# Rotating 96 images by 180 degrees: from three equal groups of images to five unlike ones

## The chip, the cores and the metric

The kernel runs on one core of one Trainium2 chip. The metric is the device time of one execution in microseconds (us); the median of several runs is given. A profile is one further execution, taken by the hardware profiler, with a time of its own.

## The reference

The input is 32 x 3 images of 256 x 256 float32 values, 25.17 MB. The output is each image turned by 180 degrees, so nothing is calculated: every byte is moved once.

```python
batch, c, h, w = 32, 3, 256, 256

def reference(x: np.ndarray) -> np.ndarray:
    return np.rot90(x, k=2, axes=(-2, -1)).astype(np.float32)
```

If an image is seen as one list of 65,536 values, turning it by 180 degrees is reversing that list.

## The kernel before

The 96 images are taken as three groups of 32. A group is a tile of 128 rows (the partitions of SBUF) by 16,384 columns: each image is cut into four segments of 16,384 values, and each segment is one row of 64 KB. The three tiles are called `A`, `Bt` and `Ct`; together they hold the whole input in SBUF, so every byte is loaded once, turned in place and stored once.

Reversing an image has two parts. The values within each row are reversed by VectorE. The four rows of an image change places (row 0 with row 3, row 1 with row 2); that is done by the store, which writes the segments of each image to DRAM in backward order (`[:, ::-1, lo:hi]`, line 58).

VectorE reverses a row by swapping columns from both ends (`swap`, lines 61 to 65): up to `J` = 2,048 columns from the right end are copied backward into the scratch tile `T`, the matching columns from the left are copied backward into the right end, and `T` is copied to the left end. So each swap is three copies, all recorded at line 52 (`copy`), and in the profile they show as `T<-A`, `A<-A` and `A<-T`. `turn(t, lo, hi)` repeats this for a range of columns of the left half. The copies keep the order in which they are written.

DMAs are issued from two queues: SP's (`nc.sync`), which carries nearly everything, and ACT's (`nc.scalar`), which loads `Bt` only. Loads are all recorded at line 55 and stores at line 58. The order is written out by hand at the end of the function:

- lines 69 to 71: `A` and `Ct` are loaded by SP, `Bt` by ACT, each as a whole;
- lines 80 and 81: `A` is turned but for its last 2,048 columns of the half; then a small store of `A` is issued, 256 columns (`LEAD`) of each row, 128 KB in all;
- lines 82 to 84: the first 1,008 columns (`MID`) of `Bt` are turned, then the rest of `A`, and the rest of `A` is stored;
- lines 85 to 88: the rest of `Bt` is turned and stored, then `Ct` is turned and stored.

All stores are issued by SP, in this order, each after VectorE has finished the columns it reads. A store has two sides. The side in SBUF is 128 rows. The side in DRAM is a list of three levels: images, segments of an image in backward order, and columns. In the built program it has the form 32x4x256 for the small store, 32x4x16128 for the rest of `A`, and 32x4x16384 for `Bt` and `Ct`. The side in DRAM of a load is 128 rows in order.

Of the kernel before, what the change touches and what calls it, by code (L numbers as in the profile page):

```python
# [2 lines left out]

os.environ.setdefault("NEURON_RT_ULTRASERVER_MODE", "4")

# [4 lines left out]


@with_exitstack
def kernel(
    ctx: ExitStack,
    tc: tile.TileContext,
    x: bass.AP,
    out: bass.AP,
):

    nc = tc.nc
    P = 128

    B, C, H, W = x.shape
    L = H * W
    G = 32
    E = L // 4
    J = E // 8

    x4 = x.rearrange("b c h w -> (b c) (h w)").rearrange(
        "(g n) (s e) -> g (n s) e", n=G, s=4)
    o4 = out.rearrange("b c h w -> (b c) (h w)").rearrange(
        "(g n) (s e) -> g n s e", n=G, s=4)  # L40

    pool = ctx.enter_context(tc.tile_pool(name="slots", bufs=1))
    A = pool.tile([P, E], x.dtype, tag="A")
    Bt = pool.tile([P, E], x.dtype, tag="B")
    Ct = pool.tile([P, E], x.dtype, tag="C")
    T = pool.tile([P, J], x.dtype, tag="T")

    def back(t, lo, hi):
        return t[:, hi - 1:(lo - 1 if lo else None):-1]

    def copy(dst, src):
        tc.keep_in_program_order(nc.vector.tensor_copy(out=dst, in_=src))  # L52

    def load(t, g, lo, hi, queue=nc.sync):
        return queue.dma_start(out=t[:, lo:hi], in_=x4[g][:, lo:hi])

    def store(t, g, lo, hi):
        return nc.sync.dma_start(
            out=o4[g][:, ::-1, lo:hi], in_=t[:, lo:hi])

    def swap(t, lo, w):
        hi = E - lo - w
        copy(T[:, 0:w], back(t, hi, hi + w))
        copy(t[:, hi:hi + w], back(t, lo, lo + w))
        copy(t[:, lo:lo + w], T[:, 0:w])

    MID = 1008
    LEAD = 256
    load(A, 0, 0, E)
    load(Bt, 1, 0, E, nc.scalar)  # L70
    load(Ct, 2, 0, E)

    def turn(t, lo, hi):
        while lo < hi:
            w = min(J, hi - lo)
            swap(t, lo, w)
            lo += w

    half = E // 2
    turn(A, 0, half - J)  # L80
    store(A, 0, 0, LEAD)
    turn(Bt, 0, MID)
    turn(A, half - J, half)
    store(A, 0, LEAD, E)
    turn(Bt, MID, half)
    store(Bt, 1, 0, E)
    turn(Ct, 0, half)
    store(Ct, 2, 0, E)


# [1 line left out]
_INS = ['x']  # L92
_OUTS = [((32, 3, 256, 256), 'float32')]


# [23 lines left out]
```

## Time and profile before

| | |
|---|---|
| median of 3 runs | 121.99 us (121.83 to 122.44) |
| the profiled execution, its own time | 122.31 us |
| its span, first to last instruction | 120.5 us |
| VectorE busy | 44.7 us (37%), 39 copies |
| moved by DMA | 50.33 MB in 1,008 packets, mean 418 GB/s |
| small store of `A`: issued, landed after | 45.77 us, 16.3 us |
| rest of `A`: issued | 59.28 us |

How to read it: times are counted from the start of the span. The page cuts the span into 40 equal slices of 3 us and prints one digit for each: the share of the slice, in tenths, in which an engine was busy; for DMA it is the mean of the core's 16 DMA engines. The rows of the DMA queues (`q1` is SP's, `q10` is ACT's) say how many packets and bytes each carried, and how much of 16 engines' time over the span they took. The rows of the issues say for each transfer which tile it writes from which (`out_dram<-A` is a store of `A`), its size where the page has it, and the time from issue to landing. An issue to landing contains all the time that the transfer waits in the queue behind earlier ones. A row of 64 KB makes one packet, and the 112 packets under 512 B carry no data of the images but close the transfers.

### The profile page before, as it was taken

The page shows a single profiled execution, that of the slowest core. Times are in us where ns is not written, and L with a number is a line of the kernel's source. Part 1 is how long each engine was busy: PE and PEld are TensorE (multiplying, and loading weights), DVE is VectorE, ACT ScalarE, POOL GpSimd, SP SyncE. Part 2 cuts the span into 40 slices and gives each one's busy share as a digit, 9 for nine tenths or more (in the row PEclk, how much of TensorE's full clock was granted, in tenths as well). Part 3 has the DMA queues.
Part 4 walks back from the last instruction along what each step waited for, and adds up shares of the span by engine and source line. Part 5 has one row for each costly group of instructions (what it writes and reads, how often), then busy time and mean ns, then how long its engine had stood idle before and what let it go on. Part 6 is the DMA issues. An engine that isn't in the chain of part 4 may idle for free.

```text
span 120.5 us, 96 instructions
## 1 busy us (share of the span) xinstructions
DVE 44.7 (37%) x39; POOL 0.2 (0%) x4
## 2 busy tenths in 40 slices
DVE  0000000000000099999999999999910000000000
POOL 0000000000000000000000000000000000000000
DMA  9888988898889888988999977988898889888980
GB/s 348 348 348 370 674 348 348 370 652 370 348 370 652 370 348 348 674 370 348 348 386 599 428 343 343 664 369 348 348 674 370 348 348 674 370 348 348 674 370 0
DMA packets 1008, 50.33 MB, mean 418 GB/s; under 512 B 112, under 2 KB 240, under 8 KB 240
## 3 DMA queue, kind: packets, MB, share of 16 engines
q1 hardware_dynamic: 864, 41.94, 81.3%
q10 hardware_dynamic: 144, 8.39, 16.1%
HBM read 25.17 MB, written 25.17 MB: 418 GB/s over the span
## 4 chain that ended last, share of the span: by engine, by line
DVE 37%; DMA 34%; issue 1%
DMA A<-in_x_dram 34%; DVE T L52 12%; DVE Bt L52 9%; DVE A L52 8%; DVE Ct L52 8%
## 5 line engine op out<-in xcount | busy, mean ns | idle before, releaser
L52 DVE COPY T<-A 128x2048 f32<-128x2048 f32 x4 | 4.9, 1227 | 42.1 <-DMA A<-in_x_dram 42.0
L52 DVE COPY Bt<-T 128x2048 f32<-128x2048 f32 (+2 forms) x5 | 5.1, 1014 | 0.2
L52 DVE COPY T<-Bt 128x2048 f32<-128x2048 f32 (+2 forms) x5 | 5.1, 1014 | 0.2
L52 DVE COPY Bt<-Bt 128x2048 f32<-128x2048 f32 (+2 forms) x5 | 5.1, 1013 | 0.2
L52 DVE COPY T<-Ct 128x2048 f32<-128x2048 f32 x4 | 4.9, 1228 | 0.1
L52 DVE COPY A<-T 128x2048 f32<-128x2048 f32 x4 | 4.9, 1227 | 0.1
L52 DVE COPY Ct<-T 128x2048 f32<-128x2048 f32 x4 | 4.9, 1227 | 0.1
L52 DVE COPY Ct<-Ct 128x2048 f32<-128x2048 f32 x4 | 4.9, 1227 | 0.1
L52 DVE COPY A<-A 128x2048 f32<-128x2048 f32 x4 | 4.9, 1226 | 0.1
L103 POOL MEMSET const-bfloat16-1.0<- 128x1 bf16 x1 | 0.1, 101 | 0.0
L103 POOL MEMSET const-uint8-127<- 128x1 uint8 x1 | 0.1, 101 | 0.0
L103 POOL MEMSET const-float32-0.0<- 128x1 f32 x1 | 0.1, 98 | 0.2 <-issue 0.2
L103 POOL MEMSET const-float32-1.0<- 128x1 f32 x1 | 0.1, 98 | 0.0
## 6 DMA issues: line engine op xcount, KB each, us to landing
out_dram<-A SPq DMA_DIRECT2D x1, 8064.0 KB, 21.9
out_dram<-A SPq DMA_DIRECT2D x1, 128.0 KB, 16.3
Bt<-in_x_dram ACTq DMA_DIRECT2D x1, 41.4
A<-in_x_dram SPq DMA_DIRECT2D x1, 41.2
Ct<-in_x_dram SPq DMA_DIRECT2D x1, 60.5
out_dram<-Bt SPq DMA_DIRECT2D x1, 27.6
out_dram<-Ct SPq DMA_DIRECT2D x1, 31.8
```

The costliest lines, as they stand in the source:

```text
L52: tc.keep_in_program_order(nc.vector.tensor_copy(out=dst, in_=src))
L103: nc = _bacc.Bacc("TRN2", target_bir_lowering=False, num_devices=1)
```

## The change

The three equal groups become five unlike ones, of 8, 32, 32, 16 and 8 images, called `a` to `e`. Each group is again a tile of 128 rows, so an image of `a` and `e` is cut into 16 rows of 4,096 values (16 KB), one of `b` and `c` into 4 rows of 16,384 (64 KB), and one of `d` into 8 rows of 8,192 (32 KB). In the profile all five tiles are called `tile`.

The loads are issued in the order `a` (SP), `e` (ACT), `b`, `c`, `d` (SP). VectorE turns `a`, `e`, most of `b` (all but the last 1,152 columns of its half), the first 2,912 columns of `c`, the end of `b`, the rest of `c`, and `d`. The stores are issued in the order `b`, `c`, `d`, `a`, `e`, all by SP and each as a whole; there is no small store ahead of them. In the built program the DRAM sides of the stores have the forms 32x4x16384 (`b`, `c`), 16x8x8192 (`d`) and 8x16x4096 (`a`, `e`); the SBUF sides are 128 rows. VectorE has 42 copies instead of 39. `J` is 2,048 as before.

```diff
-    MID = 1008
-    LEAD = 256
-    load(A, 0, 0, E)
-    load(Bt, 1, 0, E, nc.scalar)
-    load(Ct, 2, 0, E)
+    class Group:
+        def __init__(self, name, first, count):
+            rows = P // count
+            self.width = L // rows
+            self.tile = pool.tile([P, self.width], x.dtype, tag=name)
+            self.source = images[first:first + count].rearrange(
+                "n (s e) -> (n s) e", s=rows)
+            self.target = turned[first:first + count].rearrange(
+                "n (s e) -> n s e", s=rows)
+
+        def load(self, queue):
+            queue.dma_start(out=self.tile[:, :], in_=self.source)
+
+        def store(self):
+            nc.sync.dma_start(out=self.target[:, ::-1, :], in_=self.tile[:, :])
...
-    half = E // 2
-    turn(A, 0, half - J)
-    store(A, 0, 0, LEAD)
-    turn(Bt, 0, MID)
-    turn(A, half - J, half)
-    store(A, 0, LEAD, E)
-    turn(Bt, MID, half)
-    store(Bt, 1, 0, E)
-    turn(Ct, 0, half)
-    store(Ct, 2, 0, E)
+    counts = (("a", 8), ("b", 32), ("c", 32), ("d", 16), ("e", 8))
...
+    a.load(nc.sync)
+    e.load(nc.scalar)
+    b.load(nc.sync)
+    c.load(nc.sync)
+    d.load(nc.sync)
+
+    LAST = 1152
+    MID = J + 864
+    half = b.width // 2
+    a.turn(0, a.width // 2)
+    e.turn(0, e.width // 2)
+    b.turn(0, half - LAST)
+    c.turn(0, MID)
+    b.turn(half - LAST, half)
+    b.store()
+    c.turn(MID, half)
+    c.store()
+    d.turn(0, d.width // 2)
+    d.store()
+    a.store()
+    e.store()
```

More of the change, by code (lines that the diff above doesn't have):

```diff
@@ L32, with turn @@
     L = H * W
[L33 to L40, printed above, removed]
+    J = L // 32
+    images = x.rearrange("b c h w -> (b c) (h w)")
+    turned = out.rearrange("b c h w -> (b c) (h w)")
     pool = ctx.enter_context(tc.tile_pool(name="slots", bufs=1))
-    A = pool.tile([P, E], x.dtype, tag="A")
-    Bt = pool.tile([P, E], x.dtype, tag="B")
-    Ct = pool.tile([P, E], x.dtype, tag="C")
     T = pool.tile([P, J], x.dtype, tag="T")
+    class Group:
[11 more added lines that the diff above has]
+            nc.sync.dma_start(out=self.target[:, ::-1, :], in_=self.tile[:, :])
+        def turn(self, lo, hi):
+            while lo < hi:
+                w = min(J, hi - lo)
+                swap(self.tile, self.width, lo, w)
+                lo += w
     def back(t, lo, hi):
@@ L52, in copy, with swap @@
         tc.keep_in_program_order(nc.vector.tensor_copy(out=dst, in_=src))
[L54 to L62, printed above, removed]
+    def swap(t, width, lo, w):
+        hi = width - lo - w
         copy(T[:, 0:w], back(t, hi, hi + w))
@@ L65, in swap @@
         copy(t[:, lo:lo + w], T[:, 0:w])
-    MID = 1008
-    LEAD = 256
-    load(A, 0, 0, E)
-    load(Bt, 1, 0, E, nc.scalar)
-    load(Ct, 2, 0, E)
[L73 to L77, printed above, removed]
-    half = E // 2
-    turn(A, 0, half - J)
-    store(A, 0, 0, LEAD)
-    turn(Bt, 0, MID)
-    turn(A, half - J, half)
-    store(A, 0, LEAD, E)
-    turn(Bt, MID, half)
-    store(Bt, 1, 0, E)
-    turn(Ct, 0, half)
-    store(Ct, 2, 0, E)
+    counts = (("a", 8), ("b", 32), ("c", 32), ("d", 16), ("e", 8))
+    groups, first = [], 0
+    for name, count in counts:
+        groups.append(Group(name, first, count))
+        first += count
+    a, b, c, d, e = groups
+    a.load(nc.sync)
[18 more added lines that the diff above has]
+    e.store()
 _INS = ['x']
```

## The prediction

> **What bounds the kernel now.** I read the page from its second part down: how busy each engine and the DMA are over time, then what the DMA queues carried, then when each DMA was issued and when it landed, and last the trace's busy time by stage. The page first: the DMA row and the packet totals, the two queues, and the issues.
>
> ```profile
> DVE  0000000000000099999999999999910000000000
> ...
> DMA  9888988898889888988999977988898889888980
> ...
> DMA packets 1008, 50.33 MB, mean 418 GB/s; under 512 B 112, under 2 KB 240, under 8 KB 240
> ...
> q1 hardware_dynamic: 864, 41.94, 81.3%
> q10 hardware_dynamic: 144, 8.39, 16.1%
> ...
> out_dram<-A SPq DMA_DIRECT2D x1, 8064.0 KB, 21.9
> ...
> Bt<-in_x_dram ACTq DMA_DIRECT2D x1, 41.4
> A<-in_x_dram SPq DMA_DIRECT2D x1, 41.2
> Ct<-in_x_dram SPq DMA_DIRECT2D x1, 60.5
> out_dram<-Bt SPq DMA_DIRECT2D x1, 27.6
> out_dram<-Ct SPq DMA_DIRECT2D x1, 31.8
> ```
>
> VectorE works in the middle third only (44.7 us of 120.5). The DMA digits are 8 or 9 almost from edge to edge, and the queue shares add up to 81.3 + 16.1 = 97.4% of sixteen engines' time. So the kernel is bound by bytes over sixteen DMA engines, and only 3 us of the span are not their work. The next view is busy time by stretches (columns: stretch, length, VectorE, GpSimd, clock, DMA share, GB/s). A share above 1 in a short stretch comes from whole packets counted where they start.
>
> ```profile
> 0.00:1.70 1.70, 0.00 (x0) 0.20 (x4) 1.00 0.00 0
> ...
> 80.30:99.60 19.30, 7.44 (x7) 0.00 (x0) 1.00 0.99 428
> 99.60:118.90 19.30, 0.00 (x0) 0.00 (x0) 1.00 0.99 431
> 118.90:120.50 1.60, 0.00 (x0) 0.00 (x0) 1.00 0.01 0
> ```
>
> The store stages stand at 0.99; what is idle is 1.7 us at the start and 1.6 at the end. The third view is the timeline, which has the issue times (start, length, instruction):
>
> ```profile
> 41.99 1.23 DVE L52 COPY T<-A 128x2048 f32<-128x2048 f32 x1 [41.99 <-DMA A<-in_x_dram]
> 43.25 1.23 DVE L52 COPY A<-A 128x2048 f32<-128x2048 f32 x1
> ...
> 72.84 0.54 SPq L58 DMA_DIRECT2D out_dram<-Bt  x1
> ...
> 87.98 0.54 SPq L58 DMA_DIRECT2D out_dram<-Ct  x1
> ```
>
> Issue plus time to landing gives the stages. Ct's load, issued at 1.18, lands at 61.7: that is the whole of the reading, 25.17 MB. A's large store, issued at 59.28, lands at 81.2; Bt's at 72.84 + 27.6 = 100.4; Ct's at 87.98 + 31.8 = 119.8. So 8.39 MB of stores take 19.3 us on sixteen engines, 2.3 us per MB. From the last landing to the profiled execution's 122.31 us are 2.5 us. The chain of waits names A's load and then VectorE, but that is the chain by releasers; the DMA never runs dry behind it.
>
> **Loads, part by part.** The bytes are the same: 8 + 32 + 32 + 16 + 8 images make 25.17 MB in and out. Loads go out in the order a (SP) beside e (ACT), then b, c, d. Before, 16.78 MB in two queues had landed at 42.0, from a first movement at 1.7: 2.4 us per MB. So a and e, 4.19 MB, land at about 12, b at 31, c at 51, d at 61 to 62. Nothing of this moves the end of reading: 61.7 stays. One more issue ahead of b on SP (0.4 us each) happens while a moves.
>
> **VectorE.** It has 42 copies instead of 39, over the same number of elements. A 128x2048 copy repeats every 1.26 us (43.25 - 41.99). The turns: a 3.8 and e 3.8 us (done by 20); b's first part 9 x 1.26 plus three copies of 896 at about 0.65 (the 1008 ones take 0.69) = 13.3, from 31 to 45; c's first part 3.8 + 1.9 = 5.7, from 51 to 57; b's last 1152 columns 3 x 0.80 = 2.4, to 59 to 60. Then b's store is issued. Its cover is the end of reading: before, SP issued the first load at 0.73 and nothing moved until 1.7, so about 1 us of start makes 60 to 61, against a last landing of 61.7. It just fits; each us that this store came later would be a us at the end. I take 0, with 0 to +0.8. c's turn is done near 69 and needed at 81, d's near 77 and needed at 100; a and e were ready long before. VectorE's earlier start therefore buys nothing: no DMA waits for it.
>
> **The removed lead store.** It is 128 rows of 1 KB. Reading's end to A's landing is 81.2 - 61.7 = 19.5 us, against 19.3 for an unsplit store: the lead costs 0.2 us, and goes.
>
> **Shorter rows.** Loads and stores of a and e are 512 rows of 16 KB where 128 of 64 KB were; those of d 256 of 32 KB where 128 were: 512 rows more. If a row more costs what the lead's did (0.2 us for 128), that is 0.8; if the bytes alone count, 0. Eight KB and more stand nearer to the 64 KB rows than to 1 KB, so I take 0.2. With the lead's 0.2 this cancels.
>
> **The stores of a and e.** All depends on this part. In the built order the last two stores have the form 8x16x4096, d's is 16x8x8192, those of b and c 32x4x16384. Every DMA of before has an outermost count of 32 or 128, and 112 packets under 512 B for seven DMAs is 16 each: one closing packet on each of sixteen engines. So a list with a multiple of 16 at its head is seen to be spread over sixteen. A list that begins with 8 isn't in the trace. Bounds: if the 128 rows are dealt out all the same, a and e take 4.19 / 8.39 x 19.3 = 9.65 us, and the cost is 0. If each outer entry goes to one engine, eight engines carry what sixteen did: 19.3 us, or +9.65. A gain is excluded, since sixteen engines at 0.99 are the most there is. A further end: two streams that share a path take twice as long (A and Bt shared the engines up to 42 and landed together at 42, while 8.39 MB alone take 19.3). Should the eight engines be slowed so as well, it is 38.6 us, or +28.95. Nothing hides any of this: a and e are last, and both would sit on the same eight engines, so engines that ended d's share early find no more work. I take +9.65: all that the trace has is even shares of whole outer entries, eight entries make eight such shares, and 16 KB rows ran nowhere at half speed.
>
> [...]
>
> [...]
>
> **The sum.** Reading ends at 61.7; b 19.3 and c 19.3; d 9.65; that is 110.0. Then a and e 19.3: 129.3. With the 2.5 us of the end, 131.8 for an execution that corresponds to the profiled 122.31. That one is 0.3 above the median of 121.99, so **131.5**.
>
> **Rivals.**
>
> *Sixteen engines after all* (not slower). The rows are dealt out whatever the list looks like. For it: all seven DMAs of before ended on sixteen engines, though their lists differ (32 and 128). Against it: both are multiples of 16. It decides if the two last stores close with 16 small packets each. Then 110.0 + 9.65 + 2.5 - 0.3 = 121.9, with 121.3 to 122.8 by the small terms: the DMA was full before and is full after. Chance 0.13.
>
> *Eight engines, each at half speed.* For it: streams on one path do halve each other, as A and Bt did. Against it: before, all sixteen engines together ran stores at 428 to 431 GB/s without loss, so no shared path below that is seen. 110.0 + 38.6 + 2.5 - 0.3 = 150.8; with a part of the slowing, anything between 132 and 151. Chance 0.23.
>
> *d's store suffers too*, its 16 entries being slowed like the eight: another 9.65, 141 to 160. For it speaks only that 16 is a new count; it is a multiple of 16. Chance 0.05.
>
> **How the numbers follow.** The forecast, eight engines at full speed, has 0.59; its own range is 130.5 to 133 (row and cover terms of -0.4 to +1.4). Range 130 to 152: it holds the forecast, the halving and what lies between; left out are the sixteen engines (0.13) and the worst of d (some 0.04). What a measurement can tell from no change is 0.5%, 0.6 us. Faster by more than that needs the sixteen engines and a row cost of nothing: 0.03. Within it, the rest of that rival: 0.10. Slower: 0.87.
>
> **What would show it.** In the changed kernel's profile: b's store issued at 59 to 60 and landed near 81, c's near 100, d's near 110; first copy near 12; the two last landings about 9.65 us apart, the last near 129; the DMA row at 9 up to about 110 and at 4 to 5 for some 19 us after it. Packets under 512 B: 8 x 16 + 2 x 8 = 144 with eight engines, 160 with sixteen. DMA digits of 2 in the end would mean the halving; a b store that lands well after 81, a lost cover. The prediction is wrong if the last stretch stands at 9, or if the time is lost before a's store begins.

## The result and the profile after

The changed kernel takes 148.76 us (median of 4 runs, 148.70 to 150.18), the kernel before 122.22 us beside it (4 runs, 121.83 to 122.68). The ratio is 1.221, with a 95% interval of 1.216 to 1.226: slower by 26.5 us, where 9.5 were forecast. The profiled execution took 148.77 us, its span is 147.0.

The page of the changed kernel, in the order in which the page of before was read:

```profile
DVE  0004950019994099999990000000000000000000
...
DMA  5999998979696999996969696969699945444530
...
DMA packets 1424, 50.33 MB, mean 342 GB/s; under 512 B 144, under 2 KB 144, under 8 KB 144
...
q1 hardware_dynamic: 1280, 48.24, 84.2%
q10 hardware_dynamic: 144, 2.10, 3.5%
...
out_dram<-tile SPq DMA_DIRECT2D x1, 4096.0 KB, 42.7
out_dram<-tile SPq DMA_DIRECT2D x2, 2048.0 KB
```

A slice is now 3.7 us. VectorE begins at 13 us instead of 42 and is done by 77: its part went as planned. The DMA row stays high up to slice 32, about 118 us, and then falls to 4 and 5: half of the engines are idle. There are 144 small packets for ten transfers, 8 x 16 + 2 x 8: two transfers closed on eight engines. These two print no time to landing on the page, but the completion events in the trace have it: `a` landed at 135.4 us and `e` at 146.1.

The place of the loss is plainer in the stretches (columns: stretch, length, VectorE, GpSimd, clock, DMA share, GB/s):

```profile
80.40:100.00 19.60, 0.00 (x0) 0.00 (x0) 1.00 1.03 435
100.00:110.00 10.00, 0.00 (x0) 0.00 (x0) 1.00 0.94 197
110.00:119.00 9.00, 0.00 (x0) 0.00 (x0) 1.00 1.01 233
119.00:128.00 9.00, 0.00 (x0) 0.00 (x0) 1.00 0.51 149
128.00:137.00 9.00, 0.00 (x0) 0.00 (x0) 1.00 0.49 188
137.00:146.00 9.00, 0.00 (x0) 0.00 (x0) 1.00 0.31 129
```

The first line is the store of `c`: sixteen busy engines, 435 GB/s. The next two are the store of `d`: the share says that all sixteen engines are as busy as before, but they move half as much. That is the reading to take from this page: **share and rate have to be read together**, because an engine counts as busy for the whole of a slow packet. The 32 KB packets of `d` took 2.52 us here (median); in `flat_all`, an experiment below that stores `d` at full rate, they took 1.21. The last three lines are `a` and `e`: half of the engines, and at first less than half of the rate.

Landings say the same. These are the issues of `c` and `d` and the time to landing of `c`; that of `d`, 42.7, is on the page above:

```profile
69.78 0.56 SPq L55 DMA_DIRECT2D out_dram<-tile  x1
out_dram<-tile SPq DMA_DIRECT2D x1, 30.9
77.35 0.57 SPq L55 DMA_DIRECT2D out_dram<-tile  x1
```

The store of `b` is issued at 59.78 and lands 21.3 later, at 81.1; that of `c` lands at 69.78 + 30.9 = 100.7; that of `d`, issued at 77.35, at 120.05. So `d` took 19.4 us, where 4.19 MB of `b` or `c` take 9.65. The end, 2.5 us before 148.77, is at 146.3: `a` and `e` took 26.2 us. By the completion events that is some 15.4 us for `a` and 10.7 for `e`.

### The profile page after: what moved, and what is told of

Its sections match the earlier page's. It is cut to its first block, busy times and chain, and to the rows that moved or that the text cites. A ratio compares the mean times of both kernels' runs of the same rounds, so it can differ in the third digit from the quotient of the medians.

```text
span 147.0 us, 105 instructions
## 1 busy us (share of the span) xinstructions
DVE 45.1 (31%) x42; POOL 0.2 (0%) x4
## 4 chain that ended last, share of the span: by engine, by line
DMA 34%; DVE 17%; SPq 1%; issue 1%; DVEq 0%
DMA tile<-in_x_dram 34%; DVE tile L67 11%; DVE T L67 6%; SPq L52 1%; DVEq L67 0%
## 5 line engine op out<-in xcount | busy, mean ns | idle before, releaser
L67 DVE COPY T<-tile 128x2048 f32<-128x2048 f32 (+4 forms) x14 | 15.0, 1074 | 31.2 <-DMA tile<-in_x_dram 30.8
L67 DVE COPY tile<-T 128x2048 f32<-128x2048 f32 (+4 forms) x14 | 15.0, 1075 | 0.5
L67 DVE COPY tile<-tile 128x2048 f32<-128x2048 f32 (+4 forms) x14 | 15.0, 1074 | 0.5
## 6 DMA issues: line engine op xcount, KB each, us to landing
out_dram<-tile SPq DMA_DIRECT2D x1, 4096.0 KB, 42.7
```

## The experiments

The theory after this result: the list at the head of a store decides which engine walks which rows (theory L in the expectations), and engines that read the same part of SBUF hold each other up, as if two of them, a pair, had one path (theory P). Both are guesses of the author's: no trace shows which rows an engine takes, or a path. The rivals: that short rows are slow, that only the number of engines counts, that DRAM is the side that is slow.

### Is it the lists or the short rows?

`flat_all` stores `a`, `d` and `e` with their 128 rows in forward order, so the segments of these images do not change places:

```diff
+        def store_forward(self):
+            nc.sync.dma_start(out=self.forward, in_=self.tile[:, :])
...
-    d.store()
-    a.store()
-    e.store()
+    d.store_forward()
+    a.store_forward()
+    e.store_forward()
```

`self.forward` is the same piece of DRAM as 128 rows in order.

> The changed kernel, but the stores of a, d and e write the 128 rows in forward order, so that their DRAM side is 128 rows and not 16x8 or 8x16; the segments of these images do not change places. Loads, turns, bytes, row lengths and the order of issues stay. Theory L (the list at the head of the store sets which engine walks which rows, and some of them hold each other up): d at 9.65 us instead of the 19 that its packets show, a and e at 9.65 instead of 26.8, so 148.8 - 9.5 - 17.2 = 122 (121.3 to 123), with 160 packets under 512 B. Rival R (short rows of 16 and 32 KB are slow to store): 146 to 149.

Measured: 122.54 us, 1.0035 times the kernel before (1.0015 to 1.0054), 160 small packets. All 26 us are gone, with the same rows of 16 and 32 KB. The short rows are acquitted; with everything else that the change brought (three more transfers in all, though the small store is gone) they cost 0.4 us. `flat_all` changes the direction of these three stores with their lists. Direction alone is not the cause: `b` and `c` are stored backward at full rate (422 and 435 GB/s in the changed kernel), and `each_image`, below, stores forward and is slow.

`flat_ae` does this for `a` and `e` only, `flat_d` for `d` only.

> Only the stores of a and e write their rows forward (their segments do not change places); d's store stays 16x8x8192. Theory L: d keeps its 19 us, a and e fall from 26.8 to 9.65: 131.6, and packets of 32 KB stay near 2.5 us. Rival E (the whole loss comes from eight engines, d is only late through them): 122, packets of 32 KB at 1.2 us.

> Only d's store writes its rows forward (its segments do not change places); those of a and e stay 8x16x4096. Theory L with a fixed price for each list: 148.8 - 9.5 = 139.3. If a and e took 26.8 us only because d left the engines in step or apart, they take anything from 19.3 (eight engines at full speed: 131.8) to 38.6 (eight engines at half speed: 151). 144 packets under 512 B in each case.

Measured: `flat_ae` 133.56 us (ratio 1.094, 1.090 to 1.098), `flat_d` 141.55 us (1.160, 1.156 to 1.164), each some 2 us above the sum with fixed prices (131.6 and 139.3). Against `flat_all`, `d`'s list alone costs 11.0 us and the lists of `a` and `e` alone 19.0. Together that would be 30.0, while the changed kernel lost 26.2 against `flat_all`: the two are not simply added. That `d` is only late through the eight engines is refuted: `d` is slow when `a` and `e` are not, and its stretch in `flat_ae` looks as it did in the changed kernel:

```profile
90.00:100.00 10.00, 0.00 (x0) 0.00 (x0) 1.00 1.13 452
100.00:110.00 10.00, 0.00 (x0) 0.00 (x0) 1.00 0.88 187
110.00:120.00 10.00, 0.00 (x0) 0.00 (x0) 1.00 1.01 231
```

In `flat_d` the store of `d` runs at full rate, and the stage of `a` and `e` follows it:

```profile
100.00:110.00 10.00, 0.00 (x0) 0.00 (x0) 1.00 1.02 426
110.00:119.00 9.00, 0.00 (x0) 0.00 (x0) 1.00 0.48 111
119.00:128.00 9.00, 0.00 (x0) 0.00 (x0) 1.00 0.52 151
128.00:138.00 10.00, 0.00 (x0) 0.00 (x0) 1.00 0.43 170
```

At a share of 0.48, eight engines should move about half of 426, or 213. They move 111 at first, so each runs at half speed (the median 16 KB packet takes 1.26 us in this stretch, 0.62 in `flat_all`), and they get faster later.

### DRAM or SBUF, and the number of engines

The next two kernels start from the kernel before, whose stores of `Bt` and `Ct`, in rows of 64 KB, ran at 428 and 431 GB/s, and divide the store of `Ct`. `ct_halves` makes two stores of 64 rows of it, one after the other; `ct_quarters` four of 32 rows.

```diff
-    store(Ct, 2, 0, E)
+    for r in (0, 1):
+        nc.sync.dma_start(out=o4[2][16 * r:16 * r + 16, ::-1, :],
+                          in_=Ct[64 * r:64 * r + 64, :])
```

```diff
-    store(Ct, 2, 0, E)
+    for r in range(4):
+        nc.sync.dma_start(out=o4[2][8 * r:8 * r + 8, ::-1, :],
+                          in_=Ct[32 * r:32 * r + 32, :])
```

> The kernel before, but the store of Ct is issued as two stores of 64 rows, 16x4x16384 each. The DRAM side is as it was: images 256 KB apart, four segments of 64 KB each backward; sixteen engines. Only the partitions that are read at a time change. [...] Rival D (DRAM: sixteen images written in step, 256 KB apart): no change, 122, since the same addresses are written in the same sizes.

> [...] Theory P: each engine runs at full speed, packets of 64 KB at 2.42 us, and only the eight idle engines cost: 122 + 19.3 = 141.3, the same as the two halves, by the other mechanism. Rival (a store over few partitions is slow by itself): packets near 5 us and 180. Packets under 512 B: 6 x 16 + 4 x 8 = 128.

Measured: 142.36 us (ratio 1.165, 1.162 to 1.168) and 141.44 us (1.159, 1.155 to 1.162); the author's estimate for either was 141.3. Nearly the same price twice, and the stretches show that it is paid in two ways. First the halves, then the quarters:

```profile
100.00:110.00 10.00, 0.00 (x0) 0.00 (x0) 1.00 1.05 216
110.00:120.00 10.00, 0.00 (x0) 0.00 (x0) 1.00 0.96 210
120.00:130.00 10.00, 0.00 (x0) 0.00 (x0) 1.00 1.02 210
```

```profile
100.00:110.00 10.00, 0.00 (x0) 0.00 (x0) 1.00 0.48 210
110.00:120.00 10.00, 0.00 (x0) 0.00 (x0) 1.00 0.49 210
120.00:130.00 10.00, 0.00 (x0) 0.00 (x0) 1.00 0.48 210
```

On 64 rows sixteen engines are busy all the time (share 0.96 to 1.05) and move 210 to 216 GB/s, each packet of 64 KB taking some 5.1 us. On 32 rows eight engines (share 0.48 to 0.49) move the same 210 GB/s, with a median packet of 2.42 us. Eight more engines and 32 more rows brought nothing. A slow transfer over few rows is thus refuted as a rival. DRAM is an unlikely one: `ct_halves` writes the addresses of the kernel before in the same packets from as many engines, and eight engines on eight images at a time are at full speed in `ct_quarters` (210 GB/s at a share of 0.48) and at half speed when `flat_d` begins to store `a` (111 GB/s at 0.48). What surely differs is which rows of SBUF are read at a time. But no run shows which addresses are written at the same time, so DRAM is not strictly excluded.

### Sixteen engines on sixteen rows

`each_image` starts from the changed kernel and stores `a` and `e` image by image, in forward order (segments do not change places):

```diff
+        def store_each(self):
+            rows = P // self.target.shape[0]
+            for n in range(self.target.shape[0]):
+                nc.sync.dma_start(out=self.target[n],
+                                  in_=self.tile[n * rows:(n + 1) * rows, :])
...
-    a.store()
-    e.store()
+    a.store_each()
+    e.store_each()
```

> The stores of a and e are issued image by image: 16 stores of 16 rows of 16 KB, forward (segments of an image do not change places), 16 neighbouring partitions each; everything else as changed. [...] Rival E (only the count of engines matters): 9.65 us for a and e, 131.6. Small packets: 8 x 16 + 16 x 16 = 384 with sixteen engines each.

Measured: 144.06 us (ratio 1.180, 1.169 to 1.192), 384 small packets, so sixteen engines per store. `d` landed at 77.66 + 43.3 = 121.0; the end, 2.5 us before the profiled 144.62, is at 142.1. `a` and `e` took 21 us, against 26.2 with eight engines and 9.65 at full speed.

```profile
120.00:131.00 11.00, 0.00 (x0) 0.00 (x0) 1.00 0.80 207
131.00:141.00 10.00, 0.00 (x0) 0.00 (x0) 1.00 0.84 169
```

Not all of the 21 us comes from slow packets. The last eight stores were issued only from 122.96 us on, as earlier ones landed, and shares of 0.80 and 0.84 mean that engines stood idle for part of the time. The first eight, all issued by 121.3 us, are free of this: by the completion events they had landed at 132.2, 11.2 us after `d`, where full speed is 4.8, and 16 KB packets took 1.06 us on average meanwhile, against 0.62 in `flat_all`. So the number of engines alone is refuted. What sets the 1.06 us, between the 0.62 of full speed and the 1.26 at which `flat_d` began to store `a`, is not shown.

### Loads

`ct_load_halves` is the kernel before with the load of `Ct`, not its store, in two halves of 64 rows:

```diff
-    load(Ct, 2, 0, E)
+    for r in (0, 1):
+        nc.sync.dma_start(out=Ct[64 * r:64 * r + 64, :],
+                          in_=x4[2][64 * r:64 * r + 64, :])
```

> The kernel before, but the load of Ct is issued as two loads of 64 rows. Theory P, if writes into SBUF share paths as reads do: each half takes 19.3 us instead of 9.65, the end of reading moves from 61 to about 80, and the time to 141. If only reads of SBUF share: 122, with the cost of one more issue hidden.

Measured: 143.24 us (ratio 1.172, 1.169 to 1.175). While `Ct`'s second half was loaded, the engines were busy all the time and moved half:

```profile
61.00:71.00 10.00, 9.72 (x9) 0.00 (x0) 1.00 1.01 210
71.00:80.00 9.00, 2.42 (x4) 0.00 (x0) 1.00 1.03 211
```

So writing 64 rows of SBUF was as slow here (210 and 211 GB/s) as reading them in `ct_halves` (210 to 216).

### Two queues

`ct_halves_two_queues` issues the two halves of `ct_halves` at once, the lower by SP and the upper by ACT:

```diff
-    store(Ct, 2, 0, E)
+    for r, queue in ((0, nc.sync), (1, nc.scalar)):
+        queue.dma_start(out=o4[2][16 * r:16 * r + 16, ::-1, :],
+                        in_=Ct[64 * r:64 * r + 64, :])
```

> The kernel before, but Ct's store is issued as two stores of 64 rows at once, the lower rows by SP and the upper rows by ACT. Each engine alternates between the two queues' packets. Theory P with engines in step: both halves of a pair take the lower packet at the same time, 141 and packets near 5 us, as with two stores on one queue. If the pairs fall out of step (one on the lower rows while the other is on the upper ones), each has a path of its own: packets at 2.42 us and 122 to 126. A rule by which only the number of partitions of one store counts gives 141.

Measured: 140.39 us (ratio 1.150, 1.147 to 1.154). A second queue saves 2 us of 20. ACT's half did not wait for SP's stores and ran among the rows of `Bt`, whose store then landed at 72.72 + 44.6 = 117.3 instead of 100. So most of the loss stays, and this run can't say whether any two engines fell out of step.

### Is there something to gain at all?

Three kernels tried for the early start and the missing small store without new lists. `a_on_both_queues` loads `A` first, half of its columns by each queue, and stores each tile as a whole once it is turned:

```diff
-    load(A, 0, 0, E)
-    load(Bt, 1, 0, E, nc.scalar)
+    load(A, 0, 0, E // 2)
+    load(A, 0, E // 2, E, nc.scalar)
+    load(Bt, 1, 0, E)
...
-    turn(A, 0, half - J)
-    store(A, 0, 0, LEAD)
-    turn(Bt, 0, MID)
-    turn(A, half - J, half)
-    store(A, 0, LEAD, E)
-    turn(Bt, MID, half)
+    turn(A, 0, half)
+    store(A, 0, 0, E)
+    turn(Bt, 0, half)
```

> The kernel before with three equal groups, but A is loaded first as two halves of its columns, one by each queue, then Bt and Ct by SP; the small store of 128 KB goes, and each tile is turned and stored as a whole. It is what the change wanted (an early first tile, no small store) without new lists. Theory L: A lands near 22, its store stands in SP's queue by 38, no gap at the end of reading: 0.3 to 0.7 us less than before, 121.5 to 121.9. If the small store cost nothing: 122.2.

Measured: 123.39 us (ratio 1.010, 1.008 to 1.013): slower by 1%, a miss. `A` landed at 22.8 and its store was issued at 37.9 as expected, 24 us ahead of its turn in the queue. But the last load now landed later: 1.65 + 60.9 = 62.6 against 61.7. Whether the waiting store did this or the other order and shape of the loads is not shown. The two other kernels leave only the small store out, `no_small_store_late` with `MID` at 1,264:

```diff
-    LEAD = 256
...
-    store(A, 0, 0, LEAD)
...
-    store(A, 0, LEAD, E)
+    store(A, 0, 0, E)
```

> The kernel before, only without the small store of 128 KB: all of A is stored at once, at the place of the large store (issued at about 59.3). Theory T (at the end of reading, a store that already stands in the queue holds up the last load packets, by 0.35 us with 1 KB rows and by 1.0 us with 64 KB rows in the runs so far, and by nothing if it is issued as reading ends): the small store's 0.3 us go and the hold-up shrinks to 0 to 0.35: 0.3 to 0.7 us less than before, ratio 0.994 to 0.998. Rival (the small store covers a gap at the end of reading): the DMA stands idle for up to 1 us and the time is 0.3 to 1 us more, ratio 1.002 to 1.008.

> As the last one, with 1,264 columns of Bt turned ahead of A's last ones instead of 1,008, so that A's store is issued 0.45 us later, at about 59.75, where the changed kernel issues its first store. Theory T: no hold-up of the last loads, 0.4 to 0.7 us less than before; if the issue is now too late by some tenths, as much of that is lost again. Rival: 0.5 to 1.3 us more than before.

Measured: 122.08 us (ratio 0.9997, 0.9981 to 1.0012) and 122.25 us (1.0021, 1.0007 to 1.0035). The issues of `no_small_store` show that its last load, issued at 1.16, landed at 61.2:

```profile
Ct<-in_x_dram SPq DMA_DIRECT2D x1, 60.0
out_dram<-A SPq DMA_DIRECT2D x1, 21.5
```

Reading ended 0.5 us earlier in the profile than before, but that is no sign of a hold-up: in `ct_halves_two_queues`, which has the small store and the loads of the kernel before, the last load landed just as early, at 1.18 + 60.1 = 61.3.

```profile
Ct<-in_x_dram SPq DMA_DIRECT2D x1, 60.1
```

The timed gain of 0.3 to 0.7 us didn't come; nor did the loss that the rival expected. Neither theory is borne out, and no version beat the kernel before.

## Why the prediction was wrong, point by point

- **The bound** was right. `flat_all` has the same loads, turns and bytes and comes to 122.54; nothing but the DMA's time moved the end.
- **Loads and VectorE** were right: first copy at 12.90 (12 forecast), `b`'s store issued at 59.78 (59 to 60) and landed at 81.1 (81), `c` at 100.7 (100). The cover of `b`'s store held, and VectorE's earlier start bought nothing.
- **Lead and short rows** were set against each other at 0; `flat_all` measures the net at +0.4 us, with more in it than these two. `no_small_store` finds no price of the lead: 122.08 against 122.03.
- **Eight engines** for `a` and `e` were right: 144 small packets, and a share of 0.49 to 0.51 where the store of `c` stood at 1.03.
- **The step that failed is `d`**, taken at 9.65 us from `b`'s row because 16 is a multiple of 16. Landing to landing it took 19.4. The rival "d's store suffers too" had a chance of 0.05, since its count of engines looked safe; its bounds, 141 to 160, hold the result. The count was safe. What the runs showed in place of this step is sixteen busy engines that moved half: by its list alone `d` cost 11.0 us, and in `ct_halves` a packet took 5.1 us instead of 2.42 with nothing changed but that 64 rows are stored at a time and not 128. Whether `d` is slow for the same reason no run shows. The prediction had a measured halving, that of `A` and `Bt`, for its rival on the eight engines of `a` and `e`; for the sixteen of `d` it had nothing like it.
- **The second failure is the speed of the eight**: 19.3 us at full speed were taken, 26.2 were needed. "16 KB rows ran nowhere at half speed" was an argument from a trace that had no such rows. The halving rival gave 150.8 us, close to the result for the wrong reason: it put all of the loss on `a` and `e`, while 9.75 us of it were `d`'s.
- **Two signs** misled. Digits of 2 were to mean the halving, but `flat_d` shows half speed (111 GB/s) at a share of 0.48: its slow packets, of 1.26 us instead of 0.62, counted as busy. And the two last landings were 10.7 us apart, near the 9.65 forecast, while the time had been lost in `d` and `a`.
- **The narrow ranges** don't follow from their small terms: -0.4 to +1.4 makes 131.1 to 132.9 and 121.5 to 123.3, not 130.5 to 133 and 121.3 to 122.8. Nothing turned on it.

With the two sizes put in, the sum closes: 131.8 + 9.75 for `d` + 6.9 for `a` and `e` = 148.5, against the profiled 148.77. The result lay inside the range, near its end, but the forecast was too small by 17.3 us.

Why `d` is slow is not shown. In the trace of the changed kernel its median 32 KB packet takes 2.52 us; at 110 us, half way, six take 1.21 to 1.23, as at full rate in `flat_all`. The nearest case is `ct_halves`, where sixteen busy engines also moved half, but there a store reads 64 rows and here 128. No run shows which rows an engine takes, and it is open why 32x4 is free of the loss.

Not settled either is why `a` and `e` get faster as they go. The rates of that stage rise over time (111, 151, 170 GB/s in `flat_d`; 149, 188 and a falling end in the changed kernel), `e` takes less than `a` (10.7 us after 15.4), and `a` and `e` cost less after a slow `d` than after a fast one (26.2 us, against 28.7 in `flat_d`). That engines fall out of step as they go, in the slow `d` too, would fit all three, but it is a guess of the author's: no kernel that sets them apart on purpose was tried.

## What to carry to other kernels

In this kernel, bound by DMA, the shape of a store was part of its price, beside its bytes: lists headed by 32 or 128 over all 128 rows ran at 422 to 435 GB/s, those headed by 16 at 187 to 233, those headed by 8 at 111 to 188. Cutting the tiles into unlike groups changed these lists while every byte stayed, so look at the form of each DMA in the built program before pricing it from another row. And read the DMA share and GB/s of a stretch together: here a share of 1 at half the rate meant packets that took twice as long (32 KB in 2.52 us instead of 1.21, for `d`), and a share of 0.48 at half the rate (210 GB/s in `ct_quarters`) meant idle engines.

## What the runs showed of the hardware that was not expected

- Sixteen engines that stored 64 neighbouring rows moved 210 to 216 GB/s (`ct_halves`), no more than the 210 of eight engines that stored 32 (`ct_quarters`). Loads into 64 rows moved 210 and 211 GB/s too (`ct_load_halves`, second half).
- A list headed by 16, over all 128 rows, kept sixteen engines busy (share 0.94 to 1.01) at 197 to 233 GB/s in the changed kernel, where one headed by 32 moved 435.
- Of two stores in turn on eight engines, the second was the faster in the changed kernel: 10.7 us for `e` after 15.4 for `a`.
